# Transposing the cross-attention's residual rows and probabilities on VectorE, in blocks of 32 by 32

## The chip, the core and the metric

The kernel runs on one core of one Trainium2 chip. The core has a matrix engine (TensorE, PE in the profile; PEld is its weight load), VectorE (DVE), ScalarE (ACT), GpSimd (POOL) and SyncE (SP), which issues most of the DMAs; the DMAs run on 16 DMA engines between HBM and the on-chip memory SBUF, 128 partitions wide. Matmul results land in PSUM, from where VectorE or ScalarE take them. Each engine works through its own instructions in order and waits on semaphores for the others. The metric is the device time of one execution in microseconds, the median over several runs.

## The reference

One layer of a streaming encoder on x of 2048 tokens by 1024, in fp32: token mixing (a windowed attention and a gated recurrence side by side), cross-attention into 256 memory tokens, and a SwiGLU feed-forward part, each with a norm before and after. What the change touches is the cross-attention:

```python
h = h + rms_norm(y, g_mix_post[l])          # y: output of the token mixing
u = rms_norm(h, g_x_pre[l])
m = rms_norm(mem, g_mem[l])
y = cross_attention(u, m, wq_x[l], wk_x[l], wv_x[l], wo_x[l])
h = h + rms_norm(y, g_x_post[l])

def cross_attention(u, m, wq, wk, wv, wo):  # 4 heads of 256
    q, k, v = u @ wq, m @ wk, m @ wv        # split into heads
    p = softmax(q @ k.T * 256 ** -0.5)
    return (p @ v) @ wo
```

## The kernel before

**What is multiplied.** The kernel folds the weights of the cross-attention with the memory tokens ahead of time: a 1024 x 1024 matrix `qk` (query weights times keys, all four heads side by side) and a 1024 x 1024 matrix `vo` (values times output weights). The scores of a token are then its residual row times `qk`, and the cross-attention's output is its 1024 probabilities times `vo`. Each fp32 operand is split into a high and a low part (`split2`: ScalarE copies to the rounded high part at line 985, VectorE subtracts for the low part at line 988), and each product of two operands takes three matmuls (lines 1122 to 1124).

**The stages.** After the token mixing come large products over the same scheme, one after the other: *mixed* (output projection, `mixed_block`), *score* (times `qk`, `score_block`), *value* (times `vo`, `value_block`), then the feed-forward part (`hidden_blocks`, `down_block`). Each of the first three has 8 blocks of two row tiles (a row tile is 128 tokens by 1024). In a block the left operand, two row tiles, is streamed: `streamed` loads two raw tiles of 128x1024 (`sraw`), and a Strassen-Winograd scheme (`seven`) makes from them sums (`combine`, line 1097) and seven split operands (`made`, S tiles). The right operand is held in split T tiles, which are prepared for the next stage while the current one runs (`resident`, `half`). A block is seven steps of twelve matmuls; the first or last block of a stage can have eight products. S tiles are made two steps ahead of their use (`upto(need[g + 2])`).

**What follows a product.** The results of a block are finished one block later: `after()` of a block is a generator of which each step of the following block takes one piece. For a mixed block: the norm factors (GpSimd), the scaled rows plus x (lines 1529 and 1530), their store to `h1_d`, the mean squares (line 1476, ScalarE), and then, tile by tile, the transposition of the residual rows and their store to `h1t_d`. For a score block: the maxima and exponentials as the products come out (lines 1557, 1561, 1563, 1565), the reciprocals and the scaling (lines 1571 and 1573), and then, tile by tile, the transposition of the probabilities and their store to `pt_d`. The next stage streams from these two tensors, since a matmul needs the left operand with the summed index on the partitions.

**The transposition.** `transposed` takes a row tile as eight pieces of 128x128. TensorE transposes four of them into a PSUM bank (line 1381), ScalarE copies the bank back (line 1382), twice; the result overwrites the row tile. The stored tile of 128 partitions by 1024 goes out in one DMA (line 78), 4 KB from each partition. Value blocks use `transposed` too, for the operand of the feed-forward part; those calls are not in the diff.

**Buffers and order.** Row tiles come from a pool of 12 (`row_tile`), raw stream tiles from one of 4 in these stages, S tiles from one of 5. The order of instructions on each engine is set when the program is built, by a scheduler that runs over the whole program. Loads (line 75) and stores (line 78) go through SyncE's queue in order; a load waits there for its buffer, a store for its data.

Of the kernel before, what the change touches and what calls it, by code (L numbers as in the profile page):

```python
# [11 lines left out]
F32 = mybir.dt.float32  # L12
# [6 lines left out]
P = 128  # L19
T = 2048  # L20
D = 1024
# [8 lines left out]
NT = T // P  # L30
# [18 lines left out]
class Layer:  # L49
# [24 lines left out]
    def load(self, dst, src):  # L74
        self.nc.sync.dma_start(dst, src)
# [85 lines left out]
    def run(self):  # L161
        tc, nc, I = self.tc, self.nc, self.I
        self._n = 0
        self.last = {}
        kw = dict(reuse_waits="tile")
        self.z_d = tc.dram_tile([DIN, T], F32, name="z_d")

        self.y_d = tc.dram_tile([NT, P, D], F32, name="y_d")
        self.un_d = tc.dram_tile([KT, P, TB], F32, name="un_d")
        self.h1t_d = tc.dram_tile([NT, P, D], F32, name="h1t_d")  # L170
        self.pt_d = tc.dram_tile([NT, P, D], F32, name="pt_d")
        self.h1_d = tc.dram_tile([T, D], F32, name="h1_d")
        self.h2_d = tc.dram_tile([T, D], F32, name="h2_d")
        self.qk_d = tc.dram_tile([D, D], F32, name="qk_d")
        self.vo_d = tc.dram_tile([D, D], F32, name="vo_d")
        self.u_d = tc.dram_tile([KT, P, T], F32, name="u_d")
        self.h_d = tc.dram_tile([NFF, P, T], F32, name="hid_d")
        self.y2_d = tc.dram_tile([T, D], F32, name="y2_d")
        with (
            tc.tile_pool(name="cst", bufs=1) as self.cst,  # L180
            tc.tile_pool(name="sm", bufs=3, **kw) as self.sm,
            tc.tile_pool(name="edge", bufs=1, side="right") as edge,
        ):
            self.consts()

            for pool in (self.cst, edge):
                nc.gpsimd.memset(pool.tile([P, 24], F32, name="pad"), 0.0)
            with (
                tc.tile_pool(name="gp", bufs=1, **kw) as self.gp,
                tc.tile_pool(name="big", bufs=4, **kw) as self.big,  # L190
            ):
                self.mix()
# [867 lines left out]
        for e in (mybir.EngineType.Activation, mybir.EngineType.DVE):  # L1060
            self.last[e] = next((i for i in reversed(traced) if i.engine == e), None)

    def streamed(self, load, nk, kind, engine=None, tiles=False):


        nc = self.nc
        raw = []
        for j in range(2):
            self._n += 1
            t = self.ts.tile([P, 4, 256], F32, tag="raw", name=f"sraw_{self._n}", bufs=self.raws)  # L1070
            if tiles:
                t = t.rearrange("p k c -> p (k c)").rearrange("p (i c) -> p i c", i=2)
                load(t, j)
                raw.append([t[:, i, :].rearrange("p (k c) -> p k c", k=4) for i in range(2)])
            else:
                t = t[:, :nk, :]
                load(t, j)
                raw.append([t[:, :, i * P:(i + 1) * P] for i in range(2)])
        yield None
        (a11, a21), (a12, a22) = raw  # L1080

        room = []
        if kind == "u":
            t = self.tb.tile([P, 4, 2, 4, P], F32R, tag="T", name="S_u", bufs=3)
            room += [t[:, i] for i in range(4)]

        def made(src, e):
            self._n += 1
            t = room.pop(0) if room else self.ts.tile([P, 2, 4, P], F32R, tag="S", name=f"S_{self._n}", bufs=5)
            t = t[:, :, :nk, :]  # L1090
            self.split2(src, t[:, 0], t[:, 1], engine or e)
            return t

        def combine(a, b, op):
            self._n += 1
            t = self.st_pool.tile([P, 4, P], F32, tag="sum", name=f"sum_{self._n}", bufs=3)[:, :nk, :]
            nc.vector.tensor_tensor(t, a, b, op)
            return t

        if kind in "pqu":  # L1100
            for a, e in ((a11, "P"), (a21, "A"), (a12, "P"), (a22, "P")):
                yield made(a, e)
            return
        yield made(a11, "A")
        s1 = combine(a21, a22, ALU.add)
        yield made(s1, "P")
        s2 = combine(s1, a11, ALU.subtract)
        yield made(s2, "A")
        yield made(combine(a12, s2, ALU.subtract), "A")
        yield made(combine(a11, a21, ALU.subtract), "P")  # L1110
        yield made(a12, "A")
        yield made(a22, "P")
# [260 lines left out]
    def transposed(self, y, t):  # L1373
# [8 lines left out]
            nc.scalar.activation(tv[:, 4 * q:4 * q + 4, :], ps.rearrange("p (j t) -> p j t", j=4), AF.Copy)  # L1382
        return tv

    def store_transposed(self, dst, n, tv):
        self.store(dst[:, :, n * P:(n + 1) * P].rearrange("k p t -> p k t"), tv)

# [79 lines left out]
    def tokens(self, src, n):  # L1467

        return lambda kind: self.streamed(lambda t, j: self.load(
            t, src[n:n + 2, :, 512 * j:512 * j + 512].rearrange("i p c -> p i c")), 4, kind, "A", tiles=True)  # L1470

    def mean_square(self, a, to):

        self._n += 1
        junk = self.st_pool.tile([P, 512], F32, tag="part", name=f"junk_{self._n}", bufs=3)
        self.nc.scalar.activation(junk, a, AF.Square, scale=float(D) ** -0.5, accum_out=to)  # L1476
# [34 lines left out]
    def mixed_block(self, n):  # L1511
        nc = self.nc
        y, x, ss = {}, [], []

        def out(i, j, a, b):
            if not y:
                x.extend(self.rows_of(self.I["x"], n + r) for r in range(2))
                ss.append(self.small("q_s", 4))
                if not n:
                    self.g_mix_post = self.gain(self.I["g_mix_post"])  # L1520
            if i not in y:
                y[i] = self.row_tile()
            self.squared(y[i][:, j * 512:(j + 1) * 512], a, b, ss[0][:, 2 * i + j:2 * i + j + 1])

        def after():
            r = self.rstds(ss[0])
            s2 = self.small("q_s", 4)
            for i in range(2):
                nc.vector.scalar_tensor_tensor(y[i], y[i], r[:, i:i + 1], self.g_mix_post, ALU.mult, ALU.mult)
                nc.vector.tensor_tensor(y[i], y[i], x[i], ALU.add)  # L1530
                self.store(self.h1_d[(n + i) * P:(n + i + 1) * P, :], y[i])
                yield
            yield
            for i in range(2):
                self.mean_squares(y[i], i, s2)
                yield
            r = self.rstds(s2)
            nc.gpsimd.tensor_scalar(self.r_x[:, n:n + 2], r, 1.0, None, ALU.mult)
            yield
            for i in range(2):  # L1540
                self.transposed(y[i], y[i])
                self.store(self.h1t_d[n + i], y[i])
                yield

        return self.tokens(self.y_d, n), out, after, None

    def score_block(self, n):
        nc = self.nc
        p, den = {}, {}

        def out(i, j, a, b):
            if i not in p:
                p[i] = self.row_tile()
                den[i] = self.small("x_den", 4)
            d = p[i][:, j * 512:(j + 1) * 512]
            if b is not None:
                nc.vector.tensor_tensor(d, a, b, ALU.add)
                a = d
            r = self.r_x[:, n + i:n + i + 1]
            mx = self.small("x_mx", 2)  # L1560
            nc.vector.tensor_reduce(mx, a.rearrange("p (h m) -> p h m", h=2), AX.X, ALU.max, negate=True)
            mr = self.small("x_mr", 2)
            nc.gpsimd.tensor_scalar(mr, mx, r, None, ALU.mult)
            for h in range(2):
                nc.scalar.activation(d[:, h * M:(h + 1) * M], a[:, h * M:(h + 1) * M], AF.Exp, bias=mr[:, h:h + 1],
                                     scale=r, accum_out=den[i][:, 2 * j + h:2 * j + h + 1])

        def after():
            for i in range(2):
                rd = self.small("mc", 4)  # L1570
                nc.vector.reciprocal(rd, den[i])
                for h in range(4):
                    nc.vector.tensor_scalar_mul(p[i][:, h * M:(h + 1) * M], p[i][:, h * M:(h + 1) * M], rd[:, h:h + 1])
                yield
            yield
            yield
            for i in range(2):
                self.transposed(p[i], p[i])
                self.store(self.pt_d[n + i], p[i])
                yield  # L1580

        return self.tokens(self.h1t_d, n), out, after, None

    def value_block(self, n):
        nc = self.nc
        y, ss, u, o = {}, [], {}, {}
# [41 lines left out]
                for i in range(2):  # L1628
                    yield from self.token_sums(u[i], o[i], n - 4 + i)

        return self.tokens(self.pt_d, n), out, after, None

    def hidden_blocks(self, b, f):
        nc = self.nc
# [130 lines left out]
```

## Time and profile before

| | us |
|---|---|
| median of 3 runs | 2568.96 (2566.59 to 2569.04) |
| the profiled execution | 2568.82 |
| its span in the profile | 2566.8 |

| in the span | TensorE | VectorE | ScalarE | GpSimd |
|---|---|---|---|---|
| busy, us | 2535.9 | 1753.4 | 1298.0 | 358.1 |

Rows of the profile name the line of the kernel, the engine, the operation and the tiles, written as output<-inputs without buffer numbers: `S` and `T` are the split operands, `sraw` the raw stream tiles, `sum` the Strassen-Winograd sums, `psm` and `pss` PSUM banks, `part` a product copied out of PSUM, `row` a row tile. A wait is written as the waiting instruction, an arrow, and what released it. Matmuls overlap in the pipeline, so the duration of one is longer than its share of the time; the chain of waits shows the latter. An instruction of SyncE in the profile is the issue of a DMA; the transfer lands later.

### The profile page before, as it was taken

How to read it: one execution, taken by the hardware profiler on the slowest of the kernel's cores; microseconds unless marked ns; L12 is line 12 of the kernel's file. 1: busy time of each engine (PE TensorE's matmuls, PEld its weight loads, DVE VectorE, ACT ScalarE, POOL GpSimd, SP SyncE). 2: the span in 40 equal slices, each digit the busy share in tenths (PEclk: the TensorE clock that was granted, in tenths of full speed). 3: DMA queues.
4: the chain of work that ended last, by engine and by line, in shares of the span. 5: the costliest groups of instructions: out<-in, count | busy, mean ns of one | idle time of the engine just before them, and what ended most of it. 6: DMA issues, size and time to landing. Idle time of an engine off the chain costs nothing.

```text
span 2566.8 us, 34858 instructions
## 1 busy us (share of the span) xinstructions
PE 2535.9 (99%) x12326; PEld 2125.3 (83%) x12326; DVE 1753.4 (68%) x2791; ACT 1298.0 (51%) x2715; POOL 358.1 (14%) x540
## 2 busy tenths in 40 slices
PE   9999999999999999999999999999999999999998
PEld 8888888888988888888878888888888888888886
DVE  7785488886556778687875655576666557574756
ACT  5563466665555676576663333353333335443543
POOL 4231334321301111101210000000000000000022
PEclk9999999999999999999999999999999999999999
DMA  6445755765887896666973622253565424464776
GB/s 189 148 164 170 200 164 166 231 197 163 259 280 276 300 323 206 214 214 210 331 246 115 205 91 79 79 204 124 182 201 190 156 99 178 171 190 107 228 173 156
DMA packets 357294, 486.35 MB, mean 189 GB/s; under 512 B 20352, under 2 KB 248704, under 8 KB 357120
## 3 DMA queue, kind: packets, MB, share of 16 engines
q1 hardware_dynamic: 351072, 462.11, 54.6%
q0 software_dynamic: 6048, 22.02, 4.9%
q8 instruction: 97, 1.59, 0.3%
q14 instruction: 77, 0.63, 0.1%
HBM read 317.34 MB, written 166.72 MB: 189 GB/s over the span
## 4 chain that ended last, share of the span: by engine, by line
PE 85%; DMA 5%; DVE 4%; ACT 2%; issue 2%; POOL 1%; SPq 0%; DVEq 0%; POOLq 0%; ACTq 0%
PE psm L1122 24%; PE psm L1123 23%; PE psm L1124 23%; PE psg L158 2%; PE psg L157 2%; PE psg L156 2%; PE pss L1381 1%; DMA u_d<-row 1%; DMA raw<-in_wo_x_dram 1%; DMA y_d<-sg 1%; DMA raw<-in_wv_x_dram 1%; DMA z<-in_w_out_dram 1%; DMA x<-in_w_out_dram 0%; DVE T L988 0%; DVE S L808 0%
## 5 line engine op out<-in xcount | busy, mean ns | idle before, releaser
L1123 PE MATMUL psm<-T,S 128*128 128x512 f32 x2680 | 1042.8, 390 | 1.2 <-DVE T L988 1.1
L1122 PE MATMUL psm<-T,S 128*128 128x512 f32 x2680 | 1036.5, 391 | 4.8 <-ACT part L1137 2.7
L1124 PE MATMUL psm<-T,S 128*128 128x512 f32 x2680 | 1030.0, 390 | 1.5 <-DVE S L988 1.5
L1122 PEld LDWEIGHTS psm<-T,S 128*128 128x128 f32 x2680 | 503.0, 188 | 113.4 <-ACT part L1137 5.6
L1124 PEld LDWEIGHTS psm<-T,S 128*128 128x128 f32 x2680 | 503.1, 188 | 107.3 <-DVE S L988 2.8
L1123 PEld LDWEIGHTS psm<-T,S 128*128 128x128 f32 x2680 | 503.2, 188 | 106.0 <-DVE T L988 3.4
L985 ACT ACTIVATE S<-sum 128x512 fp32r<-128x512 f32 (+1 forms) x370 | 223.7, 620 | 370.7 <-PE psm L1124 272.2
L988 DVE TENSOR_TENSOR S<-sraw,S 128x512 fp32r<-128x512 f32 (+1 forms) x315 | 211.5, 679 | 216.9 <-ACT S L985 213.7
L988 DVE TENSOR_TENSOR S<-sum,S 128x512 fp32r<-128x512 f32 (+1 forms) x388 | 259.5, 678 | 54.2 <-ACT S L985 49.1
L1137 ACT ACTIVATE part<-psm 128x512 f32<-128x512 f32 x285 | 169.1, 598 | 239.3 <-PE psm L1124 217.8
L985 ACT ACTIVATE S<-sraw 128x512 fp32r<-128x512 f32 (+1 forms) x300 | 185.2, 619 | 104.6 <-PE psm L1124 100.1
L1509 POOL DMA_DIRECT2D y_d<-row x16 | 14.1, 879 | 1077.4 <-DVE row L1695 1026.5
L988 DVE TENSOR_TENSOR T<-row,T 128x1024 fp32r<-128x1024 f32 (+1 forms) x112 | 131.3, 1187 | 41.1 <-ACT T L985 38.9
L157 PE MATMUL psg<-u,whi 128*128 128x512 f32 x320 | 127.8, 399 | 0.0
L158 PE MATMUL psg<-u,wlo 128*128 128x512 f32 x320 | 127.1, 397 | 0.0
L156 PE MATMUL psg<-u,whi 128*128 128x512 f32 x320 | 127.0, 397 | 0.0
L1476 ACT ACTIVATE junk<-row 128x512 f32<-128x512 f32 x160 | 99.7, 624 | 36.9 <-DVE row L1498 14.4
L985 ACT ACTIVATE T<-row 128x1024 fp32r<-128x1024 f32 (+1 forms) x112 | 113.7, 1034 | 6.1 <-DMA row<-d_s 3.3
L1646 DVE TENSOR_TENSOR row<-psm,part 128x512 f32<-128x512 f32 x66 | 43.7, 688 | 68.2 <-PE psm L1124 68.2
L1655 DVE TENSOR_TENSOR part<-psm,part 128x512 f32<-128x512 f32 x66 | 43.8, 688 | 60.4 <-PE psm L1124 60.2
L1695 DVE TENSOR_TENSOR row<-psm,part 128x512 f32<-128x512 f32 x72 | 49.1, 688 | 49.0 <-PE psm L1124 48.9
L812 ACT ACTIVATE S<-S,w_mn 128x256 f32<-128x256 f32 (+1 forms) x128 | 63.1, 497 | 34.3 <-DVE w_mn L808 34.0
(364 smaller groups left out, 3629.7 us busy)
## 6 DMA issues: line engine op xcount, KB each, us to landing
sraw<-in_w_gate_dram SPq DMA_DIRECT2D x44, 512.0 KB, 3.6
sraw<-in_w_up_dram SPq DMA_DIRECT2D x44, 512.0 KB, 3.7
hid_d<-row SPq DMA_DIRECT2D x44, 512.0 KB, 2.7
sraw<-hid_d SPq DMA_DIRECT2D x32, 512.0 KB, 3.9
sraw<-in_w_in_dram SPq DMA_DIRECT2D x44, 256.0 KB, 3.5
z_d<-pair SPq DMA_DIRECT2D x20, 512.0 KB, 2.9
raw<-in_w_in_dram SPq DMA_DIRECT2D x20, 512.0 KB, 4.9
z_d<-z SPq DMA_DIRECT2D x20, 512.0 KB, 3.9
```

Of the source, the lines that this page charges most:

```text
L156: nc.tensor.matmul(ps, ah, bh, start=(i == 0), stop=False)
L157: nc.tensor.matmul(ps, ah, bl, start=False, stop=False)
L158: nc.tensor.matmul(ps, al, bh, start=False, stop=(i == n - 1))
L812: nc.scalar.activation(s[:, r, o:], s[:, r, o:], AF.Exp, bias=mn[:, i:i + 1], scale=-1.0, accum_out=den[:, i:i + 1])
L985: self.nc.scalar.activation(hi, raw, AF.Copy)
L988: self.nc.vector.tensor_tensor(lo, raw, f32(hi), ALU.subtract)
L1122: nc.tensor.matmul(ps, s[:, 0, k, :], t[:, 0, k, :], start=st, stop=False, **kw)
L1123: nc.tensor.matmul(ps, s[:, 0, k, :], t[:, 1, k, :], start=False, stop=False, **kw)
L1124: nc.tensor.matmul(ps, s[:, 1, k, :], t[:, 0, k, :], start=False, stop=sp, **kw)
L1137: nc.scalar.activation(t, ps, AF.Copy)
L1476: self.nc.scalar.activation(junk, a, AF.Square, scale=float(D) ** -0.5, accum_out=to)
L1695: nc.vector.tensor_tensor(d, a, b, ALU.add)
```

## The change

Residual rows and probabilities no longer go through TensorE and ScalarE. A new helper, `blocked`, has VectorE transpose each half of a row tile (128x512) into a new row tile. VectorE's transpose works inside blocks of 32 by 32: each block is turned, but stays in its group of 32 partitions. The instruction's pattern of reading already orders the blocks along the row. What still has to move across partitions is done by the store: `store_blocked` issues four DMAs, one for each group of 32 partitions, which write runs of 128 elements (512 B) to their place in HBM. `h1t_d` and `pt_d` get the shape (row tile, half, 128, 512).

In HBM the 128 columns of a piece now stand as four groups of 32 in another order than before, so the streams that read these tensors (`blocks` in place of `tokens`) view each raw tile with the group index first, and the sums and S tiles read it in runs of 32 elements; what they write has the same order as before. `blocked` as an argument of `streamed` switches this on.

```diff
-        self.h1t_d = tc.dram_tile([NT, P, D], F32, name="h1t_d")
-        self.pt_d = tc.dram_tile([NT, P, D], F32, name="pt_d")
+        self.h1t_d = tc.dram_tile([NT, 2, P, 512], F32, name="h1t_d")
+        self.pt_d = tc.dram_tile([NT, 2, P, 512], F32, name="pt_d")
...
-    def streamed(self, load, nk, kind, engine=None, tiles=False):
+    def streamed(self, load, nk, kind, engine=None, tiles=False, blocked=False):
...
+        at = dict(a=4) if blocked else {}
+
+        def formed(t):
+            return t.rearrange("p k (a c) -> p k a c", **at) if blocked else t
...
-                raw.append([t[:, i, :].rearrange("p (k c) -> p k c", k=4) for i in range(2)])
+                raw.append([t[:, i, :].rearrange("p (a k c) -> p k a c" if blocked else "p (k c) -> p k c", k=4, **at)
+                            for i in range(2)])
...
-            self.split2(src, t[:, 0], t[:, 1], engine or e)
+            self.split2(src, formed(t[:, 0]), formed(t[:, 1]), engine or e)
...
+            t = formed(t)
             nc.vector.tensor_tensor(t, a, b, op)
...
+    def blocked(self, y):
+
+        t = self.row_tile()
+        for h in range(2):
+            hs = slice(h * 512, (h + 1) * 512)
+            self.nc.vector.transpose(t[:, hs].rearrange("p (b k j) -> p b k j", b=4, k=4),
+                                     y[:, hs].rearrange("p (k b i) -> p b k i", b=4, k=4))
+        return t
+
+    def store_blocked(self, dst, t):
+
+        for a in range(4):
+            self.store(dst[:, :, a * P:(a + 1) * P].rearrange("h (b i) s -> i (h b) s", b=4),
+                       t[a * 32:(a + 1) * 32, :].rearrange("i (g s) -> i g s", g=8))
...
+    def blocks(self, src, n):
+
+        return lambda kind: self.streamed(lambda t, j: self.load(
+            t, src[n:n + 2, j].rearrange("i p c -> p i c")), 4, kind, "A", tiles=True, blocked=True)
...
-                self.transposed(y[i], y[i])
-                self.store(self.h1t_d[n + i], y[i])
+                self.store_blocked(self.h1t_d[n + i], self.blocked(y[i]))
...
-                self.transposed(p[i], p[i])
-                self.store(self.pt_d[n + i], p[i])
+                self.store_blocked(self.pt_d[n + i], self.blocked(p[i]))
...
-        return self.tokens(self.h1t_d, n), out, after, None
+        return self.blocks(self.h1t_d, n), out, after, None
...
-        return self.tokens(self.pt_d, n), out, after, None
+        return self.blocks(self.pt_d, n), out, after, None
```

## The prediction

> **What bounds the kernel now.** I read the page first: busy shares, slices, chain.
>
> ```profile
> span 2566.8 us, 34858 instructions
> PE 2535.9 (99%) x12326; PEld 2125.3 (83%) x12326; DVE 1753.4 (68%) x2791; ACT 1298.0 (51%) x2715; POOL 358.1 (14%) x540
> PE 85%; DMA 5%; DVE 4%; ACT 2%; issue 2%; POOL 1%; SPq 0%; DVEq 0%; POOLq 0%; ACTq 0%
> ```
>
> The profiled execution took 2568.8 us, 2.0 us more than its span; the median of the runs shown is 2568.96, the same within 0.15 us. TensorE is busy almost throughout and carries the chain. A saving therefore has to come out of TensorE's own queue, and counts in full only where no other engine is close behind. So the second view is a table of two stages, the mixed blocks and the score blocks (columns: length, then busy us of PE, PEld, DVE, ACT, POOL, granted clock, DMA share, GB/s).
>
> ```profile
> 790.00:975.00 185.00, 184.91 (x877) 153.46 (x877) 141.90 (x172) 128.29 (x278) 28.93 (x58) 1.00 0.84 300
> 975.00:1136.00 161.00, 161.00 (x776) 134.44 (x775) 126.81 (x232) 105.95 (x244) 23.82 (x30) 1.00 0.67 222
> ```
>
> Every removed transpose and every added one lies in these two rows, 346 us together. There TensorE stands still for 0.1 us in all, at granted clock 1.00, so TensorE alone sets their length. VectorE comes next: 141.9 + 126.8 = 268.7 us, 78%.
>
> **What the change takes off TensorE.** The groups by line between 810 and 1140 us, then two pieces of the chain and four matmuls in a row:
>
> ```profile
> L1381 PE MATMUL pss<-ident,row 128*128 128x128 f32 x256 | 33.6, 272 | 0.0
> L1382 ACT ACTIVATE row<-pss 128x512 f32<-128x512 f32 x64 | 35.9, 596 | 0.7 <-PE pss L1381 0.4 <-ACT S L985 0.3
> ...
> 811.53 0.87 PE pss L1381 x8
> 1131.34 0.87 PE pss L1381 x8
> ```
>
> 256 transposes go: 16 row tiles in each of the two stages, eight transposes a tile. Their durations overlap (272 ns each), so the price is not 256 x 272 ns but what a group of eight holds of the chain: 0.87 us. 32 x 0.87 = 27.8 us, half in each stage. The 64 evictions by ScalarE go as well (35.9 us busy, not on the path). If nothing else moved, the stages would take 185 - 13.9 = 171.1 and 161 - 13.9 = 147.1, 318.2 in all, and the kernel 2568.8 - 27.8 = 2541.0 us.
>
> **What it puts on VectorE.** 64 transposes of 128x512, SBUF to SBUF, which the trace has no example of. The nearest rows are VectorE's elementwise work on the same shape (timeline; start, us):
>
> ```profile
> 978.24 0.68 DVE L1561 TENSOR_REDUCE x_mx<-row 128x2 f32<-128x512 f32 x1
> 978.84 0.68 DVE L988 TENSOR_TENSOR S<-sraw,S 128x512 fp32r<-128x512 f32 x1
> ...
> 981.33 1.15 DVE L1573 TENSOR_SCALAR row<-row,mc 128x256 f32<-128x256 f32 x4
> ...
> 957.28 1.22 DVE L1530 TENSOR_TENSOR row<-row,row 128x1024 f32<-128x1024 f32 x1
> 958.41 0.68 DVE L988 TENSOR_TENSOR S<-sraw,S 128x512 fp32r<-128x512 f32 x1
> ```
>
> A 128x512 instruction lasts 0.68 us but the next starts 0.60 us after it; the pitch is what a full queue pays. I take 0.60 per transpose: one pass over 512 columns, like those rows. Lower end 0.53 (two 128x256 instructions, the fastest 512 columns on VectorE: (1.15 - 0.35) / 3 = 0.27 each). Upper end 1.13, the pitch of the 1024-column row, which is what two passes over 512 columns would cost. At 0.60 it is 64 x 0.60 = 38.4 us, so VectorE wants 268.7 + 38.4 = 307.1 of the 318.2 us that TensorE would leave: 97% on average, and in the score stage 126.8 + 19.2 = 146.0 of 147.1, 99%. That is why I don't forecast the full 27.8.
>
> How busy can an in-order VectorE be before TensorE waits? Three windows bound it:
>
> ```profile
> 1220.00:1260.00 40.00, 38.49 (x181) 31.46 (x180) 36.43 (x50) 24.75 (x59) 9.67 (x12) 1.00 1.05 329
> 940.00:960.00 20.00, 20.00 (x98) 16.73 (x97) 18.00 (x20) 19.23 (x36) 3.42 (x7) 1.00 0.94 327
> 810.00:820.00 10.00, 10.00 (x50) 8.36 (x49) 10.00 (x13) 7.51 (x15) 0.00 (x0) 1.00 0.70 223
> ```
>
> For 10 us it can be at 100% and for 20 us at 90% with TensorE untouched, since the S tiles are made two steps ahead; over 40 us at 91% TensorE lost 1.5 us. What keeps it from 100% are waits for others (VectorE's waits, 790 to 1136 us; total, times, longest):
>
> ```profile
> DVE T L988 <- ACT T L985: 25.2, 11, 11.1
> DVE S L988 <- ACT S L985: 18.6, 14, 3.4
> DVE mc L1571 <- ACT row L1565: 8.1, 8, 1.4
> DVE row L1529 <- POOL q_r L1491: 7.8, 5, 1.8
> ```
>
> The first two shrink when VectorE is late and ScalarE has 36 us less to do; the last two, 15.9 us, are latencies of the softmax and of the norm and stay in part. I take a sustained share of 0.93, a little over the 0.91 of the 40 us window: 307.1 / 0.93 = 330.2 us, 15.8 less than 346. The gain is 15.8, and 12.0 of the 27.8 us are lost again to TensorE waiting for S and T. Behind a transpose in VectorE's queue stand the low halves of S and T (L988) and the sums (L1097); TensorE's next product waits for those.
>
> Each transpose now also writes a new row tile out of the 12 instead of its own, so it can wait for a store that still reads that slot; in the order of the changed program, some of them wait for DMA semaphores. The stores landed in 2.6 to 9.0 us, and a slot comes round after about a block of some 20 us: 0, unless stores get three times slower.
>
> **The reads in pieces.** S tiles and sums of the score and value blocks read their raw tiles in runs of 32 elements. Runs of 128 in a row of 256 are in the trace, in the weight streams (1400 to 2000 us), and cost nothing against whole rows (790 to 975 us):
>
> ```profile
> L988 DVE TENSOR_TENSOR S<-sraw,S 128x512 fp32r<-128x512 f32 x95 | 64.8, 691 | 83.6 <-ACT S L985 83.5
> ...
> L988 DVE TENSOR_TENSOR S<-sraw,S 128x512 fp32r<-128x512 f32 x25 | 17.1, 686 | 6.8 <-ACT S L985 6.8
> ```
>
> I take 0. Twice the time would be the other end: 7 such readers a block on VectorE x 8 blocks x 0.60 = 34 us in the score stage, which would outweigh the gain.
>
> **The stores.** One DMA of 128 rows of 4 KB becomes four of 32 partitions in runs of 512 B: 128 issues in place of 32, and 32 x (1024 - 128) = 28,672 packets more. On SyncE's queue (issue times min/median/max; waits):
>
> ```profile
> L78 SPq DMA_DIRECT2D h1t_d<-row x16: 319/333/553, 822.0 to 976.7; - x16
> L78 SPq DMA_DIRECT2D u_d<-row x16: 360/388/870, 1171.0 to 1332.5; - x16
> L75 SPq DMA_DIRECT2D qd<-z_d x64: 573/598/1429, 271.3 to 567.9; - x64
> ...
> SPq L78 <- ACT row L1382: 62.9, 23, 7.5
> SPq L75 <- DVE S L988: 43.1, 17, 9.2
> ```
>
> At 0.39 (u_d, also 512 B runs) to 0.60 us (qd, part of the partitions) an issue, 128 of them take 50 to 77 us instead of 11. These two waits alone are 106 us of SyncE standing still, which cover it. A load queued behind a store starts up to 4 x 0.60 - 0.33 = 2.1 us later; S loads run about a block ahead: 0. The tiles are read back several blocks later, so the landing time is off the path.
>
> For the DMA engines, a rate at full share is GB/s over share, here for 860 to 940, 1170 to 1330 and 270 to 330 us:
>
> ```profile
> DMA packets 9295, 25.53 MB, mean 319 GB/s; under 512 B 813, under 2 KB 813, under 8 KB 9290
> q1 hardware_dynamic: 9290, 25.47, 88.4%
> DMA packets 41693, 44.73 MB, mean 280 GB/s; under 512 B 1488, under 2 KB 33232, under 8 KB 41680
> q1 hardware_dynamic: 41680, 44.57, 84.6%
> DMA packets 18604, 11.38 MB, mean 190 GB/s; under 512 B 896, under 2 KB 18048, under 8 KB 18597
> q1 hardware_dynamic: 18597, 11.30, 68.2%
> ```
>
> 361 GB/s for long runs, 331 with four packets in five short, 279 where short runs meet loads of 64 partitions. A 524 KB tile takes 1.45, 1.58 or 1.88 us, so the change adds 0.13 to 0.43 a tile: 2 to 7 us to the 0.84 x 185 = 155 of the mixed stage. That is 157 to 162 of 171 us: tight but not over.
>
> The Trainium skill, page "SBUF — State Buffer", section on the DMA port swizzle, speaks against this edit: a range of 32 partitions reaches only 8 of 16 ports, about 218 GB/s. The slow 270 to 330 us window points the same way, without separating it from short runs. By that figure a tile would take an estimated 2.4 us and the mixed stage's DMA 171 us, all that TensorE leaves.
>
> **Rivals.**
> 1. *VectorE has room after all* and TensorE's 27.8 us come off whole: 2541. For it: ScalarE is relieved, and VectorE's largest waits are for ScalarE. Against it: 99% in the score stage.
> 2. *The share sticks at 0.88 to 0.905*, because the L988 instructions still wait for ScalarE between transposes: 307.1 / 0.905 = 339 to 307.1 / 0.88 = 349 us, a gain of 7 to a loss of 3: 2562 to 2572, mostly no change. For it: the 40 us window, where TensorE already lost time at 0.91.
> 3. *The stores become the bound of the mixed stage.* At half the long-run rate a tile takes 2.90 us, 16 x 1.45 = 23 more: 179 us of DMA, against 141.9 + 19.2 = 161.1 / 0.93 = 173 of VectorE. With 157 for the score stage that is 336 us, a gain of 10: 2558. Against it: 279 is the worst rate shown.
> 4. *Slower: a VectorE transpose of 4-byte elements is not one pass.* At 0.93 the stages keep their 346 us when VectorE wants 321.8, which is (321.8 - 268.7) / 64 = 0.83 us a transpose. From there VectorE decides: at 1.00 us it is 332.7 / 0.93 = 358, 2581; at 1.13, 341.0 / 0.93 = 367, 2590. For it: no row shows the operation. Against it: every 128x512 form on VectorE here has a 0.60 pitch.
>
> The page "VectorE: DVE Perf Modes" of the Trainium skill, section on the three transpose paths, gives 311 ns for 128x128 in bf16 on VectorE against 390 on TensorE. If that grew with the columns, 512 would be an estimated 1.24 us and rival 4 would hold; if most of it is a fixed start, the 0.60 stands. No trace here has it.
>
> **The numbers.** Forecast 2568.8 - 15.8 = 2553 (2548 at 0.53 a transpose, 2560 at 0.70): 0.43. Rival 1: 0.09. Rival 2: 0.12. Rival 3: 0.06. Rival 4, with the doubled reads of 32-element runs on the same side: 0.30. A measurement of this kernel tells 0.2%, 5 us, from no change, so faster is below 2563.8 and slower above 2574.1: faster 0.56 (forecast, rivals 1 and 3 but for 0.04 of their tails, 0.02 of rival 2), same 0.14, slower 0.30. Range 2541 to 2581, from the full gain to 1.00 us a transpose; some 0.18 is beyond it, mostly above. The forecast's own range is 2545 to 2562.
>
> **What would show it.** Right: 128 transposes left on TensorE at the old L1381 (value blocks); 64 VectorE transposes with a pitch near 0.60; VectorE over 90% busy in both stages; TensorE waiting for DVE S and DVE T there, some 12 us, where it waits for nothing now; the stages together near 330 us. Wrong: a pitch over 0.83, S or sum rows of the score stage well over 0.69, DMA share at 1.0 with TensorE waiting for raw tiles, or VectorE waiting for stores.

## The result, and the profile after

The changed kernel takes 2555.47 us, median of 6 runs (2548.88 to 2557.17), against 2566.41 (2564.83 to 2569.04) for the kernel before in the same runs: a ratio on record of 0.9947, with a 95% interval of 0.9937 to 0.9957. That is 13.6 us of 2566 (11 to 16). The two medians alone differ by 10.9 us, at the lower end of this. The profiled execution fell from 2568.82 to 2555.81 us, by 13.0, its span by 12.7.

The page of the changed kernel, the three lines that answer to those before:

```profile
span 2554.1 us, 34424 instructions
PE 2509.0 (98%) x12070; PEld 2097.9 (82%) x12070; DVE 1784.9 (70%) x2855; ACT 1268.7 (50%) x2651; POOL 365.4 (14%) x540
PE 51%; DVE 2%; ACT 1%; DMA 1%; issue 1%; POOL 0%; SPq 0%; DVEq 0%; POOLq 0%; ACTq 0%
```

(The shares of the last line add up to 56%, so no reading rests on it.) TensorE has 256 instructions fewer and is busy 26.9 us less, but stands still 14.2 us more (span less busy time: 30.9 before, 45.1 after). The difference is the gain. To see where the stops lie, here are the two stages in one window, before and then after (columns as in the prediction: length, busy us of PE, PEld, DVE, ACT, POOL, granted clock, DMA share, GB/s):

```profile
790.00:1140.00 350.00, 349.90 (x1668) 291.22 (x1668) 272.01 (x407) 236.53 (x524) 52.75 (x88) 1.00 0.76 264
```

```profile
790.00:1140.00 350.00, 339.25 (x1480) 276.42 (x1479) 314.03 (x483) 214.93 (x476) 57.72 (x91) 1.00 0.84 269
```

In 350 us TensorE stood still for 0.1 us before and for 10.75 us after, at a clock of 1.00 both times. The rest of the 14.2 us is spread over stretches outside the two stages.

The next view splits the gain between the stages, by counting TensorE's instructions from the start (length, PE busy and instructions, clock, DMA share, GB/s). First before, up to 790, 975 and 1136 us:

```profile
0.00:790.00 790.00, 773.28 (x4386) 1.00 0.63 196
0.00:975.00 975.00, 958.19 (x5262) 1.00 0.67 215
0.00:1136.00 1136.00, 1119.19 (x6036) 1.00 0.67 216
```

Then after, up to the points where TensorE has issued as many, less the 128 and 256 removed transposes:

```profile
0.00:792.00 792.00, 772.51 (x4385) 1.00 0.63 195
0.00:972.00 972.00, 944.86 (x5134) 1.00 0.68 216
0.00:1119.50 1119.50, 1091.58 (x5780) 1.00 0.70 219
```

5262 - 128 = 5134 and 6036 - 256 = 5780. TensorE enters the mixed stage 2 us later than before (792 against 790), by stops that lie ahead of every instruction of the change. The mixed stage fell from 185 to 180 us, a gain of 5 out of 13.9. The score stage fell from 161 to 147.5, a gain of 13.5 out of 13.9. At its end TensorE is 16.5 us ahead (1136 against 1119.5), at the end of the kernel 12.7, so 3.8 us go again behind 1119.5 us. (By equal counts of instructions, so to an instruction or two of 0.23 us where the order of TensorE's work differs.)

The two stages after, cut at these points, in the columns of the window above:

```profile
792.00:972.00 180.00, 172.36 (x750) 139.81 (x749) 157.48 (x202) 112.32 (x244) 31.58 (x58) 1.00 0.92 309
972.00:1119.50 147.50, 146.71 (x648) 121.20 (x647) 138.80 (x258) 92.02 (x213) 25.01 (x30) 1.00 0.77 235
```

TensorE stands for 7.6 us in the mixed stage, where VectorE is busy 87%, and for 0.8 us in the score stage, where VectorE is busy 94%; another 2.3 us of stops lie between 1119.5 and 1140 us.

What TensorE waits for in the 350 us after (us in total, times, longest); before, the same view is empty:

```profile
PE psm L1129 <- ACT S L985: 3.9, 3, 1.7
PE psm L1131 <- DVE S L988: 2.8, 3, 1.1
PE psm L1130 <- DVE T L988: 2.0, 2, 1.4
PE psm L1129 <- ACT part L1144: 2.0, 3, 0.9
```

Line numbers have moved: L1129 to L1131 are the three matmuls of a product, L1144 is ScalarE's copy of a product's first half out of PSUM. By this view over half (5.9 of 10.7 us) waits for ScalarE, whose 36 us of evictions the change took away, and 4.8 us wait for VectorE. But the engine that a wait names may itself have been waiting. One such stop, first on TensorE, then on ScalarE, then what VectorE did ahead of it (start, length, engine and line, idle time before it and what ended it):

```profile
826.47 0.39 PE L1131 MATMUL psm<-T,S 128*128 128x512 f32 x1
828.58 0.50 PE L1129 MATMUL psm<-T,S 128*128 128x512 f32 x1 [1.72 <-ACT S L985]
```

```profile
826.89 0.60 ACT L1527 ACTIVATE row<-psm 128x512 f32<-128x512 f32 x1 [2.04 <-PE psm L1131]
827.39 0.62 ACT L985 ACTIVATE S<-sum 128x512 fp32r<-128x512 f32 x1
827.91 0.62 ACT L985 ACTIVATE S<-sraw 128x512 fp32r<-128x512 f32 x1
```

```profile
822.11 1.29 DVE L1397 STREAM_TRANSPOSE row<-row 128x512 f32<-128x512 f32 x2
823.33 1.18 DVE L988 TENSOR_TENSOR T<-row,T 128x1024 fp32r<-128x1024 f32 x1
824.44 1.29 DVE L1397 STREAM_TRANSPOSE row<-row 128x512 f32<-128x512 f32 x2
...
826.23 0.68 DVE L1104 TENSOR_TENSOR sum<-sraw 128x512 f32<-128x512 f32 x1
```

ScalarE is not full here. It stands for 2.04 us at L1527, a copy that needs a product of TensorE's, and behind that copy in its in-order queue stand the splits S that TensorE needs next. When the product is done, copy and splits follow one another while TensorE has nothing. The copy is not the whole of it: the first of the two splits takes the sum that VectorE makes at 826.23, done at 826.91 behind four of the new transposes. Without the copy ahead of it this split could have started 0.48 us earlier, at 826.91 in place of 827.39, and no more. In the kernel before, the same sum was made at 821.07 and split long before the copy:

```profile
821.07 0.69 DVE L1097 TENSOR_TENSOR sum<-sraw 128x512 f32<-128x512 f32 x1
```

```profile
823.05 0.62 ACT L985 ACTIVATE S<-sum 128x512 fp32r<-128x512 f32 x1
...
826.53 0.60 ACT L1500 ACTIVATE row<-psm 128x512 f32<-128x512 f32 x1 [0.76 <-PE psm L1124]
```

So this stop, put down to ScalarE, has VectorE's transposes behind it as well.

The new instructions on VectorE (busy us, mean ns of one, idle before), and four of them in a row:

```profile
L1397 DVE STREAM_TRANSPOSE row<-row 128x512 f32<-128x512 f32 x64 | 40.5, 680 | 0.0
```

```profile
1120.85 2.48 DVE L1397 STREAM_TRANSPOSE row<-row 128x512 f32<-128x512 f32 x4
```

Four take 2.48 us, one 0.67: the pitch is (2.48 - 0.67) / 3 = 0.60 us, that of any elementwise pass over this shape.

VectorE's share and TensorE's stops can be set side by side in two windows inside the score stage and one where the stages meet:

```profile
980.00:1100.00 120.00, 120.00 (x531) 99.40 (x530) 112.26 (x216) 72.57 (x177) 22.94 (x27) 1.00 0.80 246
1000.00:1040.00 40.00, 40.00 (x178) 33.12 (x178) 38.98 (x80) 21.73 (x53) 7.79 (x8) 1.00 0.80 239
944.00:966.00 22.00, 19.12 (x80) 14.53 (x79) 22.00 (x28) 15.06 (x31) 2.89 (x7) 1.00 0.96 330
```

In the first two VectorE is busy 94% over 120 us and 97% over 40 us, and TensorE does not stop once. In the third VectorE has no gap for 22 us, and TensorE stands for 2.9 of them. The stops lie in the first mixed blocks (828 to 890 us), where the stages meet (950 to 963) and from the end of the score blocks on (1112 on).

### The profile page after: what moved, and what is told of

Same layout as the page of the kernel before. It is cut to its first block, busy times and chain, and to the rows that moved or that the text cites. A ratio compares the mean times of both kernels' runs of the same rounds, so it can differ in the third digit from the quotient of the medians.

```text
span 2554.1 us, 34424 instructions
## 1 busy us (share of the span) xinstructions
PE 2509.0 (98%) x12070; PEld 2097.9 (82%) x12070; DVE 1784.9 (70%) x2855; ACT 1268.7 (50%) x2651; POOL 365.4 (14%) x540
## 4 chain that ended last, share of the span: by engine, by line
PE 51%; DVE 2%; ACT 1%; DMA 1%; issue 1%; POOL 0%; SPq 0%; DVEq 0%; POOLq 0%; ACTq 0%
PE psm L1131 17%; PE psm L1129 17%; PE psm L1130 17%; DVE T L988 1%; DMA u_d<-row 1%; DVE S L988 0%; ACT junk L1503 0%; PE pss L1388 0%; DMA row<-d_s 0%; DMA row<-in_w_down_dram 0%; ACT T L985 0%; DVE sum L1104 0%; ACT S L985 0%; DVE row L1397 0%; DVE row L1633 0%
## 5 line engine op out<-in xcount | busy, mean ns | idle before, releaser
L1129 PE MATMUL psm<-T,S 128*128 128x512 f32 x2680 | 1034.8, 391 | 10.8 <-ACT part L1144 5.2
L1131 PE MATMUL psm<-T,S 128*128 128x512 f32 x2680 | 1030.6, 390 | 4.5 <-DVE S L988 4.5
L1129 PEld LDWEIGHTS psm<-T,S 128*128 128x128 f32 x2680 | 503.1, 188 | 122.3 <-ACT part L1144 9.0
L1131 PEld LDWEIGHTS psm<-T,S 128*128 128x128 f32 x2680 | 503.2, 188 | 111.2 <-DVE S L988 7.1
L1144 ACT ACTIVATE part<-psm 128x512 f32<-128x512 f32 x285 | 168.6, 596 | 247.1 <-PE psm L1131 223.5
```

The lines of the kernel that those rows point to most:

```text
L1129: nc.tensor.matmul(ps, s[:, 0, k, :], t[:, 0, k, :], start=st, stop=False, **kw)
L1131: nc.tensor.matmul(ps, s[:, 1, k, :], t[:, 0, k, :], start=False, stop=sp, **kw)
L1144: nc.scalar.activation(t, ps, AF.Copy)
```

## The experiments

Times of an experiment are compared as ratios with the kernel before, run on the same chip (medians there 2572 to 2574 us). Four theories stand against each other. A: VectorE is full, and the work that it was given is what TensorE waits for. B: the four stores a tile cost time. C: the waits come with the new order of instructions that every build gets from the scheduler. L, formed after the first four runs: TensorE's own transposes had covered waits for S, T and PSUM copies that were there all along, and these now show.

**e1_no_transpose.** The rows are stored by the same four DMAs, without VectorE's transposes:

```diff
-                self.store_blocked(self.h1t_d[n + i], self.blocked(y[i]))
+                self.store_blocked(self.h1t_d[n + i], y[i])
...
-                self.store_blocked(self.pt_d[n + i], self.blocked(p[i]))
+                self.store_blocked(self.pt_d[n + i], p[i])
```

> The transposes on VectorE are left out: the rows are stored as they are by the same four DMAs a tile, so the later stages compute on untransposed numbers; amount and kind of all other work is that of the changed kernel. Theory A (the 12 to 15 us that are missing from the 27.8 are VectorE's 64 x 0.60 us in its queue): VectorE is back at 78% in the two stages, TensorE loses under 3 us there, 2541 us (2538 to 2546). Rival B (the small stores and their 28,672 extra packets cost it): nothing changes, 2553 to 2557. Rival C (it is the new order of instructions that a rebuild gives, whatever the load): somewhere between, with TensorE waits of 5 us or more left in the stages.

Measured: 0.9943 (0.9927 to 0.9959), 2556.95 us: no gain over the changed kernel. The two stages in one window, and TensorE's waits there:

```profile
790.00:1140.00 350.00, 340.97 (x1480) 277.91 (x1479) 276.74 (x417) 213.94 (x476) 54.60 (x91) 0.99 0.84 272
```

```profile
PE psm L1129 <- ACT part L1144: 4.6, 1, 4.6
PE psm L1131 <- DVE S L988: 1.7, 2, 1.4
PE psm L1129 <- ACT S L985: 1.5, 2, 1.2
PE psm L1130 <- DVE T L988: 1.3, 3, 0.6
```

VectorE is back at 79% (276.74 of 350), yet TensorE still stands for 9.0 us instead of 10.75, and the time is the same. Theory A, in which most of the loss comes from VectorE's new work, does not explain the whole loss. Stage by stage it is less clear. The mixed stage here, cut as above:

```profile
792.00:972.00 180.00, 177.04 (x772) 143.96 (x772) 141.19 (x172) 116.72 (x254) 31.64 (x58) 1.00 0.94 317
```

TensorE stands for 3.0 us of it instead of 7.6, and the stops at 828 to 851 us are gone. A single stop of 4.56 us behind ScalarE's L1144, at 1111 us, takes that back. The changed kernel does not have it: there this copy ran between the exponentials at L1591, here behind them and two splits of T. So an estimated 7.6 - 3.0 = 4.6 us of the loss can be VectorE's transposes, standing in its queue ahead of what TensorE needs, hidden by another order elsewhere. The clock was 0.99 as well, some 2 us in this window by the busy time of the same 1480 instructions (340.97 against 339.25).

**e2_one_store.** One DMA of 128 partitions in runs of 2 KB per tile, the blocks left where the transpose put them:

```diff
-        for a in range(4):
-            self.store(dst[:, :, a * P:(a + 1) * P].rearrange("h (b i) s -> i (h b) s", b=4),
-                       t[a * 32:(a + 1) * 32, :].rearrange("i (g s) -> i g s", g=8))
+        self.store(dst.rearrange("h p c -> p h c"), t.rearrange("p (h c) -> p h c", h=2))
```

> The transposes stay, but each tile goes out in one DMA of 128 partitions in runs of 2 KB in place of four in runs of 512 B, so the 32x32 blocks are not put in place and the later stages compute on misplaced numbers. Theory A: no change, 2552 to 2558, and the same TensorE waits for VectorE. Rival B: 2541 to 2546, DMA share of the mixed stage down from 0.92 to about 0.88.

Measured: 0.9939 (0.9924 to 0.9954), 2557.08 us, the same as the changed kernel. The window of the two stages:

```profile
790.00:1140.00 350.00, 340.92 (x1483) 278.18 (x1482) 316.03 (x485) 215.77 (x476) 58.40 (x91) 1.00 0.78 269
```

The DMA share fell from 0.84 to 0.78 for the same bytes (269 GB/s), and TensorE's stops from 10.75 to 9.1 us. B falls as a cause of the loss. The price of the stores can be read off: (0.84 - 0.78) x 350 / 32 = 0.66 us a tile more than one store (0.55 to 0.77 with the rounding of the shares), all of it hidden.

**e3_transposed_twice.** Each half is transposed twice, 64 more VectorE instructions: `for h in (0, 1, 0, 1):` instead of `range(2)`.

> Each of the 64 transposes on VectorE is done twice, into the same tile; the result is the same. VectorE gets another 64 x 0.60 = 38 us, in all some 347 us in two stages that now take about 330. Theory A: VectorE sets the stages, 347 / 0.95 = 365 us, so 2555 + 35 = 2590 us (2578 to 2600), slower than the kernel before. Rivals B and C: under 5 us, 2555 to 2560.

Measured: 1.0025 (1.0011 to 1.0039), 2578.14 us: (1.0025 - 0.9945) x 2573 = 21 us for 38.4 us more on VectorE (0.9945 lies between the two measurements of the changed kernel, 0.9947 and 0.9944).

```profile
790.00:1140.00 350.00, 330.12 (x1399) 267.30 (x1398) 330.50 (x522) 203.54 (x454) 53.96 (x88) 0.97 0.82 259
```

TensorE stands for 19.9 us of this window, 9 more than in the changed kernel. The clock is 0.97 here, and an instruction takes 236 ns instead of 229 (330.12 / 1399, 339.25 / 1480), another 10 us; why the clock is lower is not shown. So VectorE is close behind, but only some half of the 21 us are stops. Of the 19.9 us, 11.9 wait for ScalarE's L1144 by the view, though the edit gave ScalarE nothing to do: once more the engine named need not be where a delay began.

**b1_scaling_on_scalar.** The softmax's last scaling goes from VectorE to ScalarE, to unload VectorE:

```diff
-                    nc.vector.tensor_scalar_mul(p[i][:, h * M:(h + 1) * M], p[i][:, h * M:(h + 1) * M], rd[:, h:h + 1])
+                    nc.scalar.activation(p[i][:, h * M:(h + 1) * M], p[i][:, h * M:(h + 1) * M], AF.Copy, scale=rd[:, h:h + 1])
```

> The scaling of the probabilities by the reciprocal sums (64 instructions of 128x256, 18 us) moves from VectorE to ScalarE, which has 36 us less to do than before the change; same result. Theory A: the score stage, where VectorE is at 95%, gives 4 to 8 us back: 2547 to 2552 us. Rival (ScalarE's splits of S come later, as ScalarE needs about 64 x 0.5 = 32 us for it): 2555 to 2565. Rival B: no change, 2553 to 2557.

Measured: 0.9960 (0.9948 to 0.9973), 2562.23 us: nothing gained. TensorE's longest wait there, and what ScalarE did ahead of the copy it waited for:

```profile
PE psm L1129 <- ACT part L1144: 8.2, 4, 6.7
```

```profile
1119.73 1.70 ACT L1599 ACTIVATE row<-row,mc 128x256 f32<-128x256 f32 x4
...
1122.36 1.70 ACT L1599 ACTIVATE row<-row,mc 128x256 f32<-128x256 f32 x4
1123.96 0.59 ACT L1144 ACTIVATE part<-psm 128x512 f32<-128x512 f32 x1
```

The PSUM copy stood behind the new scalings. Less work for VectorE bought nothing, and more in front of one copy on an engine busy 67% (233.78 of 350) cost TensorE 6.7 us: here the place in a queue counted for more than the share of busy time. From here on theory L is tried.

**e4_tensor_too.** The changed kernel, with the 256 transposes given back to TensorE as well, into PSUM that nobody reads:

```diff
     def blocked(self, y):
 
+        for q in range(2):
+            ps = self.bank("sh"[q])
+            for j in range(4):
+                k = 4 * q + j
+                self.nc.tensor.transpose(ps[:, j * P:(j + 1) * P], y[:, k * P:(k + 1) * P], self.ident)
         t = self.row_tile()
```

> The changed kernel, with the 256 TensorE transposes put back beside those of VectorE, into PSUM banks that nobody reads; ScalarE's copies stay out, the result is that of VectorE. The question is what 27.8 us of TensorE work cost where TensorE waits some 11 us more than before. Theory L (TensorE's transposes used to cover waits for S tiles, T tiles and the copies out of PSUM, which come from ScalarE and VectorE at their own pace): they cover 8 to 12 us again, so 16 to 20 us more than the changed kernel, within 5 us of the kernel before, and TensorE's waits in the two stages fall below 4 us. Theory A (VectorE's added 38 us are what is waited for): the same cover, but VectorE stays at 90% and more, and 2 to 4 us of waits are left. Rival C (the waits belong to this order of instructions and not to the pace): the waits stay near 11 us and the time is 27 us more than the changed kernel, 12 to 15 more than the kernel before.

Measured: 1.0016 (1.0000 to 1.0032), 2575.78 us. The window and TensorE's waits:

```profile
790.00:1140.00 350.00, 348.06 (x1655) 287.93 (x1654) 301.10 (x465) 206.43 (x459) 54.31 (x88) 1.00 0.81 258
```

```profile
PE psm L1129 <- ACT S L985: 0.8, 1, 0.8
PE psm L1131 <- DVE S L988: 0.7, 1, 0.7
PE psm L1129 <- ACT part L1144: 0.5, 1, 0.5
```

The stops fell from 10.75 to 1.9 us, though VectorE carries every instruction of the change and the stores are all there. 27.8 us of TensorE work added cost (1.0016 - 0.9945) x 2573 = 18 us; some 10 us of it ran in time that TensorE otherwise waits. C had forecast waits near 11 us and 27 us more, which did not come. L had forecast this, but A nearly the same (2 to 4 us of waits left), since the longer stages give VectorE more time too (301.10 of 350, 86%); e4 does not decide between these two. It does bound the rest of the change: VectorE's transposes, the stores and the reads in pieces, less the evictions that ScalarE no longer has, cost 0.16%, 4 us (0 to 8), as long as TensorE has its old work.

**e6_mixed_only** and **e7_score_only.** The change in one stage alone; the other stage goes back to `transposed`, `store` and `tokens` (shown for e6, with the tensor's shape and `tokens` left out):

```diff
...
-                self.store_blocked(self.pt_d[n + i], self.blocked(p[i]))
+                self.transposed(p[i], p[i])
+                self.store(self.pt_d[n + i], p[i])
...
```

> The change in the mixed stage alone: residual rows by VectorE, probabilities by TensorE and ScalarE as before. TensorE has 13.9 us less to do. Theory A: VectorE at (141.9 + 19.2) / 171 = 94% there, 2 to 4 us lost, 10 to 12 us faster than before. Theory L: each stage loses about 40% of what TensorE gives up to waits that were covered, 7 to 9 us faster than before.

> The change in the score stage alone: probabilities by VectorE, residual rows by TensorE and ScalarE as before. TensorE has 13.9 us less to do. Theory A: VectorE at 146.0 / 147.1 = 99% there, nearly all of the 12 us of loss falls here, 2 to 6 us faster than before. Theory L: 7 to 9 us faster than before, like the mixed stage.

Measured: mixed alone 0.9974 (0.9961 to 0.9986), 6.7 us gained; score alone 0.9960 (0.9945 to 0.9975), 10.3 us gained. First the window of the mixed stage's change, then that of the score stage's:

```profile
790.00:1140.00 350.00, 341.83 (x1559) 280.33 (x1557) 293.73 (x445) 223.16 (x495) 56.37 (x88) 1.00 0.79 264
```

```profile
790.00:1140.00 350.00, 345.97 (x1575) 285.15 (x1574) 292.63 (x447) 225.34 (x499) 53.18 (x88) 1.00 0.80 265
```

Of 13.9 us each, the mixed stage gives about half and the score stage three quarters; TensorE stands for 8.2 us with the first and 4.0 with the second. The intervals overlap, but the order is that of the counts above, and it is the reverse of what a full VectorE would give: the score stage was forecast at 99%, the mixed stage at 94% (161.1 of 171.1). The stops go with the edits: with the mixed change alone they lie at 825 to 886 and 948 to 960 us, as in the changed kernel, and with the score change alone there is none before 1116 us.

**b2_max_scaled_on_vector.** In L's sense a shorter chain ahead of ScalarE's exponentials: the small product of maximum and row scale moves from GpSimd to VectorE, `nc.vector.tensor_scalar(mr, mx, r, None, ALU.mult)` at L1589.

> The changed kernel, with the scaled maxima of the softmax (32 instructions of 128x2) on VectorE in place of GpSimd, so that ScalarE's exponentials wait for one engine less; same result. Theory L: ScalarE, which stood 18 us for these maxima with copies and splits queued behind, comes earlier, 2 to 5 us faster than the changed kernel, 0.992 to 0.993 of the kernel before. Theory A: VectorE gets 3 us more in its fullest stage, 1 to 3 us slower than the changed kernel.

Measured: 0.9949 (0.9932 to 0.9966), no change, a miss for L. ScalarE's wait for the maxima fell from 17.7 to 6.1 us, but a stop of 3.24 us for ScalarE's T turned up at 1115 us: the wait was not on the path, and the new order made another.

**r1_changed_again.** The changed kernel itself on the chip of the last three experiments, as their measure.

> The changed kernel once more, so that the next three stand beside it on the same chip: 0.9937 to 0.9957 of the kernel before, some 11 us of TensorE waits in the two stages.

Measured: 0.9944 (0.9930 to 0.9957), 2559.73 us, as the first time. TensorE stands for 10.4 us of the 350 us window, and seven of the eight stops of the mixed stage come back at the same places, the first three with the same lengths (1.72, 0.36 and 0.98 us). So they go with the build and are not a chance of one execution.

**b3_copy_on_vector.** The copy at L1527, at which ScalarE stood in the stop shown above, goes to VectorE: `nc.vector.tensor_copy(d, a)` for `nc.scalar.activation(d, a, AF.Copy)`.

> The changed kernel, with the product that has no second half (the copy out of PSUM at L1527, one a block) copied by VectorE in place of ScalarE; same result. In the mixed stage ScalarE stands 2.0 us in this copy waiting for TensorE with a split of S behind it, and TensorE then waits 1.7 us for that split. Theory L (waits are made by what stands in ScalarE's queue ahead of S, T and the copies): the waits of 1.72, 0.36 and 0.98 us near 828 and 849 us go, 2 to 4 us faster than the changed kernel. Theory A: VectorE gets 0.6 us a block more, some 9 us in mixed and value stage, 2 to 5 us slower.

Measured: 0.9961 (0.9948 to 0.9973), 2561.71 us; a miss for L again. The stops of 1.72 and 0.98 us shrank to 1.13 and 0.49, as they should, and with the copy gone ScalarE stood 1.01 us for VectorE's sum instead, but TensorE now stood 5.0 us for L1144 instead of 4.0, and other stops grew.

**c2_middle_of_mixed.** The VectorE path only for the four middle blocks of the mixed stage and all score blocks, where TensorE had been seen to lose little; the other mixed blocks keep TensorE's transposes and a tensor of their own, `h1t_dw`:

```diff
+        self.h1t_dw = tc.dram_tile([NT, P, D], F32, name="h1t_dw")
...
-                self.store_blocked(self.h1t_d[n + i], self.blocked(y[i]))
+                if 4 <= n < 12:
+                    self.store_blocked(self.h1t_d[n + i], self.blocked(y[i]))
+                else:
+                    self.transposed(y[i], y[i])
+                    self.store(self.h1t_dw[n + i], y[i])
...
-        return self.blocks(self.h1t_d, n), out, after, None
+        return self.blocks(self.h1t_d, n) if 4 <= n < 12 else self.tokens(self.h1t_dw, n), out, after, None
```

> VectorE transposes only in the four middle blocks of the mixed stage (n = 4 to 10) and in all of the score stage; the first and last two mixed blocks go through TensorE and ScalarE as before; same result. TensorE gets 8 x 0.87 = 7.0 us back. Theory L (the waits sit at the two ends of the mixed stage, where TensorE's transposes covered them): 6 to 7 us of waits go with it, so 0 to 2 us faster than the changed kernel, about 0.994 of the kernel before. Rival C (waits move about with every new order): 3 to 7 us slower.

Measured: 0.9943 (0.9931 to 0.9956), 2557.30 us, beside 0.9944 for r1. TensorE has 8 x 0.87 = 7.0 us more to do and the end is the same; the stops around 828 to 849 and 951 to 963 us are gone, and the one at 890 us grew from 0.92 to 2.08:

```profile
790.00:1140.00 350.00, 342.44 (x1530) 280.58 (x1529) 304.26 (x466) 220.34 (x489) 59.32 (x91) 1.00 0.82 267
```

So taking those eight tiles off TensorE is worth nothing, give or take some 5 us by the two intervals: that work fitted into waits. L says this, but A does too, since VectorE loses the eight tiles' transposes by the same edit.

**c3_without_last_score.** As c2, and the last score block goes back to TensorE too, since stops lie there as well.

> As c2, and the last score block through TensorE as well (1.7 us more TensorE work, ahead of the value stage's first waits of 0.8 to 1.2 us); same result. Theory L: the waits of 1.1 and 0.8 us at the end of the score stage go, so within 1 us of c2. Rival C: 2 us or more slower than c2.

Measured: 0.9950 (0.9937 to 0.9963), 2560.24 us: no better than c2, the intervals overlap. No version tried beat the changed kernel beyond its interval.

## Why the prediction held, and where its reasoning failed

- *TensorE loses 27.8 us.* Right: it is busy 26.9 us less.
- *A transpose on VectorE costs 0.60 us.* Right to the hundredth; rival 4, slower through a dearer transpose, falls with it. The estimate of 1.24 us from the page "VectorE: DVE Perf Modes" of the Trainium skill, section on the three transpose paths, does not hold for fp32 at 512 columns. The other reading of that figure, a mostly fixed start, does not conflict with the row.
- *The reads in runs of 32 cost 0.* Right; in the changed kernel the low halves of S and the sums that read in runs of 32 (975 to 1112 us, the score stage) average 683 and 685 ns, against 686:

```profile
L988 DVE TENSOR_TENSOR S<-sraw,S 128x512 fp32r<-128x512 f32 x22 | 14.9, 683 | 0.0
...
L1104 DVE TENSOR_TENSOR sum<-sraw,sraw 128x512 f32<-128x512 f32 x6 | 4.1, 685 | 1.0 <-DMA sraw<-pt_d 1.0
```

- *The stores are hidden.* Right (e2), but the DMA price was mis-sized: 0.66 us a tile, not 0.13 to 0.43. It lies between these and the estimated 0.95 that follows from the half-port rate in the Trainium skill's page "SBUF — State Buffer", section on the DMA port swizzle (the estimated 2.4 us less 1.45). No run separates partitions from run length. Rival 3 asked for 1.45 us more and did not come about.
- *A write to a row slot does not wait for a store.* Not quite: two instructions of ScalarE's did, a copy and, at 1006 us, an exponential (2.36 us, with no stop of TensorE's behind it), where before nothing of the kind was seen. The copy:

```profile
937.12 0.60 ACT L1527 ACTIVATE row<-psm 128x512 f32<-128x512 f32 x1 [3.23 <-DMA h1t_d<-row]
```

  A stop of 0.86 us on TensorE follows at 951 us; with one store a tile (e2) both are absent. That the one made the other is not shown. It is a matter of 1 us.
- *VectorE over 90% busy in both stages, the stages near 330 us.* Half right: VectorE was busy 87% in the mixed stage and 94% in the score stage. The stages took 327.5 us by the counts above (180 + 147.5). But the share over both is 296.28 / 327.5 = 0.905 and not 0.93, the upper end of rival 2, and VectorE's work in them came to 296.28 us (157.48 + 138.80) and not 307.1; four of the 64 transposes, which the prediction had all in these two stages, fell behind them. That 296.28 / 0.905 comes out near 307.1 / 0.93 is luck.
- *12 us are lost because VectorE cannot keep up more than 0.93 of its queue.* This is the step that failed. The size came out near, some 14.2 us (27.8 less 13.6) against 12.0, but a share of VectorE's time is not what sets the loss. The score stage, forecast at 99% and measured at 94%, lost 0.8 us to stops and gave 13.5 of 13.9 us; the mixed stage, at 87%, lost 7.6 us and gave 5. TensorE was to wait some 12 us for VectorE's S and T; it waited 4.8 us for these and 5.9 for ScalarE. Leaving out VectorE's transposes altogether (e1) did not give the loss back; putting TensorE's work back (e4) removed the stops. What the runs show in place of the share is the order of the queues: TensorE stops where what it needs stands behind something else, on ScalarE or on VectorE, and with TensorE's transposes in place these stops hardly show (0.1 us before, 1.9 in e4). One sentence of the prediction holds beside this: the sums do stand behind the transposes, at 826 us, and the stops at 828 to 851 us are absent where the transposes are left out (e1). The prediction's row with 0.1 us of idle time was read to mean that TensorE alone sets the length of the stages. It said only that TensorE always had something to do.
- *Rival 1, the full 27.8 us,* falls: 2541 was never reached, not even in e1 without VectorE's share.

What stays open is how the 10.75 us divide between VectorE's transposes, standing ahead of sums and low halves, and the order on ScalarE. No run separates A's part from L's: e1 points to some 4.6 us in the mixed stage for the transposes, and e4 and c2 fit both. That the waits were there all along, as L has it, is not shown either: at the stop above the order in both queues had changed. Open too is how much would go with another order of the same instructions. Each edit moved some stops and made others (b2, b3, c2, c3), so a shift of 1 to 4 us cannot be put down to the edit alone. More row tiles or S buffers were not tried.

## What to carry to other kernels

An engine without idle time in a stage may owe that to filler: work that needs nothing just then covers the waits of the work that does. When such work is moved away, price the saving as its length less the waits that it covered; here 27.8 us of transposes were worth some 14, and putting the same work back as a dummy showed the cover directly. And look for the next stop by who stands ahead of the needed instruction in an in-order queue, not by which engine has the largest busy share. Follow that queue one engine further than the wait's name: the stop at 828 us names ScalarE, and the late sum came from VectorE.

## What the runs showed of the hardware

A 32 by 32 block transpose of 128x512 fp32 on VectorE has a pitch of 0.60 us and lasts 0.67, as long as an elementwise pass over the same tile. Four stores of 32 partitions in runs of 512 B took some 0.66 us (0.55 to 0.77) more of the 16 DMA engines' time per 512 KB tile than one store of 128 partitions in runs of 2 KB.
